# Weight sums of a seven-product scheme: made by DMAs that add to their destination instead of by VectorE

## The chip, the cores and the metric

The kernel runs on one core of one Trainium2 chip. The metric is the device time of one execution in microseconds (us). Of the kernel before, three runs took 2652.19, 2656.02 and 2655.14 us, so the median is 2655.14 us.

## The reference, cut to what matters

The reference is a trunk of two layers on a residual stream of 512 tokens by 1024 features, all in fp32. Each layer runs a gated feed-forward block, a mixer (short convolution beside dilated attention) and a second gated feed-forward block, each on a normed and modulated copy of the stream:

```python
def _swiglu(h, w_gate, w_up, w_down):
    return (jax.nn.silu(h @ w_gate) * (h @ w_up)) @ w_down
```

Here `w_gate` and `w_up` are 1024 x 2816 and `w_down` is 2816 x 1024. There are four such blocks (two layers, two each). Only the products `h @ w_gate` and `h @ w_up` are touched by the change.

## The kernel before, in words

**Split matmuls.** TensorE works on fp32r operands. Every fp32 operand is split into a high part (`hi`, a cast by ScalarE) and a rest (`lo = x - hi`, a subtraction by VectorE), and a product is three matmuls: hi by hi, hi by lo, lo by hi.

**Seven products instead of eight.** For most of the feed-forward's 22 column blocks of 128, two blocks m and m+1 form one group, the class `Seven`. Its weights are two tiles named `raw`, each 128 x 8 x 256, one of `w_gate` and one of `w_up`. Cut into upper and lower 512 rows they give four quarters: a and c (gate), b and d (up). The activations are quartered too. Seven products of sums of quarters replace the eight plain ones. A `Product` casts and subtracts a quarter of 128 x 1024 (lines 539 and 150 of the profile), then runs 24 matmuls of 256 columns (line 550). The sums of activations are made once per block by `Sums.make`; the sums of weights are made for every group by `minus` (line 572), which writes over a quarter in its `raw` tile.

**What sets the order.** In `ffn`, `up` runs over groups and overlaps two of them: while group m runs its products 5, 6, 7, 4 and 3, the next group is loaded and runs its products 1 and 2. A part of two or three groups is followed by `down_part`, which multiplies the finished activations by `w_down`. The framework's scheduler reorders instructions of the several engines by its own estimates, after which every engine works through its list in that order and waits at semaphores. Four `raw` tiles exist (`RAWS = 4`); they hold the two weights of two groups, and `w_down` and the mixer's weights pass through the same four. Loads are issued from the SP queue.

**At the start.** `rows` (line 283) loads small vectors as rows into a tile `rows` of which there are two; TensorE turns them (line 288), VectorE copies them into `vec`. It is called three times: norms and conv weights, the bias `ada_b` of layer 0, that of layer 1.

**POOL** before the change does a few adds of squares for the norms (line 399), a power (354), some modulations (376) and copies in the attention. It issues no DMA.

Of the kernel before, what the change touches and what calls it, by code (L numbers as in the profile page):

```python
# [21 lines left out]
F32 = mybir.dt.float32  # L25
# [5 lines left out]
P = 128  # L31
D = 1024
S = 512
# [87 lines left out]
def trunk(ctx: ExitStack, tc: tile.TileContext, x, c, ada_t, ada_b, norm_g, ffn_w_gate, ffn_w_up, ffn_w_down,  # L121
# [155 lines left out]

    def rows(srcs, col):
        n = sum(s.shape[0] for s in srcs)
        st = sp.tile([P, P], F32, tag="rows", bufs=2, name="rows")  # L280
        at = 0
        for s in srcs:
            nc.scalar.dma_start(st[at:at + s.shape[0]], s)
            at += s.shape[0]

        def end():
            pt = bank("at")
            T.transpose(pt[:, :n], st[:n], ident[:n, :n])
            V.tensor_copy(vec[:, col:col + n], pt[:, :n])

        return end
# [204 lines left out]
    class Sums:  # L496
# [8 lines left out]
        def make(self, i, whole):  # L505

            h11, h21 = whole[:, :4, HALF[0]], whole[:, :4, HALF[1]]
            h12, h22 = whole[:, 4:, HALF[0]], whole[:, 4:, HALF[1]]
            dst, a, b, op = ((h22, h21, h22, ALU.add), (h22, h22, h11, ALU.subtract),
                             (h21, h11, h21, ALU.subtract), (h22, h12, h22, ALU.subtract))[i - 1]  # L510
            V.tensor_tensor(dst, a, b, op=op)
            hi, lo = (v[:, i - 1] for v in self.parts)
            A.copy(hi, dst)  # L513
            sub(lo, dst, f(hi))
# [41 lines left out]
    class Seven:  # L556

        def __init__(self, raw1, raw2, sums, tag="mm"):  # L560
            self.a, self.c = raw1[:, :4], raw1[:, 4:]
            self.b, self.d = raw2[:, :4], raw2[:, 4:]
            self.sums = sums
            self.one, self.two, self.three = bank(tag), bank("at"), None

        def kept(self, src):
            s = F.take()
            A.copy(s.ap, src)  # L568
            return s

        def minus(self, dst, x, y):
            V.tensor_tensor(dst, x, y, op=ALU.subtract)  # L572

        def plus(self, s, src):
            V.tensor_tensor(s.ap, s.ap, src, op=ALU.add)

        def split1(self):
            self.p1 = Product(self.a, quarter(0, 0), self.one, True)

        def split2(self):  # L580
            self.p2 = Product(self.c, quarter(1, 0), self.two, True)
# [5 lines left out]
        def run2(self):  # L587
            self.p2.run()
            self.plus(self.c11, self.two)

        def split5(self, room=None):
            self.minus(self.a, self.b, self.a)
            self.three = bank("o")
            self.p5 = Product(self.a, self.sums(1), self.three, True, room)

        def split6(self):
            self.minus(self.a, self.d, self.a)
            self.p6 = Product(self.a, self.sums(2), self.one)

        def run56(self):  # L600
            self.p5.run()
            self.p6.run()
            self.c12 = self.kept(self.one)

        def split7(self):
            self.minus(self.b, self.d, self.b)
            self.p7 = Product(self.b, self.sums(3), self.one)

        def run7(self):
            self.p7.run()  # L610
# [1 line left out]
            self.plus(self.c22, self.three)  # L612

        def split43(self):
            self.minus(self.c, self.c, self.a)
            self.p4 = Product(self.c, quarter(1, 1), self.one)
            self.p3 = Product(self.d, self.sums(4), self.three)

        def run43(self):
# [4 lines left out]
        def out(self):  # L624
            return self.c11, self.c12, self.one, self.c22

    def first_group(raws):

        sums = Sums()
        group = Seven(*raws, sums, "o")  # L630
        group.split1()
        group.split2()
        group.split5(sums.room())
        return group

# [14 lines left out]
    def gate_up(l, i):  # L650

        held = {}

        def raws(m):
            return [load(w[l, i][:, m * P:(m + 2) * P]) for w in (ffn_w_gate, ffn_w_up)]

        def get(m):
            if m not in held:
                g, u = (halves_of(raw, NC) for raw in raws(m))
                held[m], held[m + 1] = (g[0], u[0]), (g[1], u[1])  # L660
            return held.pop(m)

        get.held, get.raws = held, raws
        return get

    def ffn(l, i, get, first, whole):

        acts = {}
        R.top = N_LOW
        group = first_group(get.raws(len(first) + len(first) % 2))  # L670

        def swiglu(m, pg, pu):
            t = F.take()
            A.activation(t.ap, pg, AF.Silu)  # L674
            V.tensor_tensor(t.ap, t.ap, pu, op=ALU.mult)
            hi, lo = R.take(), R.take()
            A.copy(hi.ap, t.ap)
            sub(lo.ap, t.ap, f(hi.ap))
            t.give()
            acts[m] = hi, lo  # L680

        def swiglu_pair(m, g1, u1, g2, u2):

            A.activation(g1.ap, g1.ap, AF.Silu)
            V.tensor_tensor(u1.ap, u1.ap, g1.ap, op=ALU.mult)
            g1.give()
            s = F.take()
            A.activation(s.ap, g2, AF.Silu)
            V.tensor_tensor(u2.ap, u2.ap, s.ap, op=ALU.mult)
            s.give()  # L690
            hi, lo = R.take(2), R.take(2)
            hv, lv = (s.ap.rearrange("p (c n) -> p c n", c=2) for s in (hi, lo))
            for half, t in enumerate((u1, u2)):
                tv = t.ap.rearrange("p (c n) -> p c n", c=2)
                A.copy(hv[:, :, HALF[half]], tv)  # L695
                sub(lv[:, :, HALF[half]], tv, f(hv[:, :, HALF[half]]))
                t.give()
            acts[m], acts[m + 1] = zip(hi.apart(), lo.apart())

        wv = whole.ap.rearrange("p (k n) -> p k n", k=NC)  # L700
        sums = group.sums
        modulating["phase"] = "up"
        if len(first) % 2:
            for n, banks in enumerate(first):
                swiglu(n, *banks)
            banks = [any_bank() for _ in range(2)]
            for pd, u in zip(banks, get(len(first))):
                project([(pd, u)], h, NC)
            swiglu(len(first), *banks)
        group.run1()  # L710
        group.run2()
        groups = {len(first) + len(first) % 2: group}
        begun = [False]

        def make(i):
            if not begun[0]:
                sums.make(i, wv)

        def up(part):
            modulating["phase"] = "up"  # L720
            late = None
            for m in range(*part):
                if m not in groups:
                    continue
                here, after = groups.pop(m), None
                if not begun[0]:
                    make(1)
                    here.split6()
                    make(2)
                    if len(first) % 2 == 0:  # L730
                        for n, banks in enumerate(first):
                            swiglu(n, *banks)
                else:
                    here.split5()
                    here.split6()
                    if late:
                        swiglu_pair(*late)
                if m + 2 < DFF // P:
                    after = groups[m + 2] = Seven(*get.raws(m + 2), sums)
                    after.split1()  # L740
                here.run56()
                make(3)
                here.split7()
                if after:
                    after.run1()
                    after.split2()
                here.run7()
                here.split43()
                make(4)
                if after:  # L750
                    after.run2()
                here.run43()
                if not begun[0]:
                    begun[0] = True
                    whole.give()
                late = m, *here.out()
                if not after:
                    sums.give()
                    R.top = N_R
            if late:  # L760
                swiglu_pair(*late)

        def rhs(lo):
            return lambda k: (acts[lo + k][0].ap, acts[lo + k][1].ap)

        def down_part(part):
            modulating["phase"] = "down"
            lo, hi = part
            down(ffn_w_down[l, i][lo * P:hi * P], rhs(lo), hi - lo, (l, 2 * i, 2))
            for m in range(lo, hi):  # L770
                for s in acts.pop(m):
                    s.give()

        for part in FF_PARTS[:-2]:
            up(part)
            down_part(part)
        up(FF_PARTS[-2])
        up(FF_PARTS[-1])
        down_part(FF_PARTS[-2])
        lo, hi = FF_PARTS[-1]  # L780

        def give():
            for m in range(lo, hi):
                for s in acts.pop(m):
                    s.give()

        return ffn_w_down[l, i][lo * P:hi * P], rhs(lo), mods[l, 2 * i, 2], give
# [665 lines left out]
```

## Time and profile before

| | |
|---|---|
| median of three runs | 2655.14 us |
| profiled execution, whole | 2655.01 us |
| its span | 2653.2 us |
| PE (matmul) busy | 2615.4 us, 99% |
| DVE busy | 1835.8 us, 69% |
| ACT busy | 1174.3 us, 44% |
| POOL busy | 212.0 us, 8% |
| DMA queue q1, share of 16 engines | 37.3% |

Busy times are read against the span; time outside the span is 1.8 us. A matmul's busy time overlaps that of the next, so the time that PE stands still is read from its waits and from the starts of its instructions.

### The profile page before, as it was taken

What the parts mean: (1) busy time and instruction counts of PE and PEld (TensorE: products, weight loads), DVE (VectorE), ACT (ScalarE), POOL (GpSimd) and SP (SyncE); (2) the same over time, 40 slices, a digit from 0 to 9 for tenths busy, and PEclk for the clock granted to TensorE, in tenths of its full rate; (3) what the DMA queues carried; (4) which work ended last, traced back from release to release, by engine and by line L of the source; (5) the groups of instructions that cost most, each with busy time, mean ns of one, the idle gap of its engine ahead of it and who ended that gap; (6) DMA issues with size and microseconds to landing.
All of it is one profiled execution on the core that took longest, in us unless ns stands there. A gap on an engine that the chain in (4) does not pass through costs nothing. (4 is left out here: it accounts for less than half of the span.)

```text
span 2653.2 us, 40548 instructions
## 1 busy us (share of the span) xinstructions
PE 2615.4 (99%) x16265; PEld 2347.4 (88%) x16265; DVE 1835.8 (69%) x2867; ACT 1174.3 (44%) x2200; POOL 212.0 (8%) x545
## 2 busy tenths in 40 slices
PE   8999999999999999999999999999999999999998
PEld 6899989888888889999999999988888888999998
DVE  8987775675672468877888777756756634777675
ACT  5444454353352345444564445443444423545343
POOL 0000022011010020000020000311112000200001
PEclk9999999999999999999999999999999999999999
DMA  9544143352342224353414423443523422233221
GB/s 328 189 160 129 55 145 120 127 160 87 127 136 87 95 88 145 126 190 101 155 65 167 151 96 114 133 123 98 178 90 118 143 83 84 64 112 101 91 92 68
DMA packets 285480, 326.42 MB, mean 123 GB/s; under 512 B 8057, under 2 KB 263404, under 8 KB 285292
## 3 DMA queue, kind: packets, MB, share of 16 engines
q1 hardware_dynamic: 284980, 323.71, 37.3%
q8 instruction: 127, 2.08, 0.3%
q14 instruction: 61, 0.50, 0.1%
q10 hardware_dynamic: 312, 0.13, 0.0%
HBM read 321.67 MB, written 2.13 MB: 122 GB/s over the span
## 5 line engine op out<-in xcount | busy, mean ns | idle before, releaser
L220 DVE TENSOR_TENSOR slots_r<-raw,slots_r 128x512 fp32r<-128x512 f32 (+1 forms) x584 | 364.9, 644 | 322.3 <-PE mm L241 158.1
L219 ACT CAST slots_r<-raw 128x512 fp32r<-128x512 f32 (+2 forms) x584 | 326.6, 582 | 406.1 <-PE mm L242 174.8
L240 PE MATMUL mm<-hh,slots_r 128*128 128x512 f32 (+1 forms) x1320 | 485.9, 370 | 0.0
L241 PE MATMUL mm<-hl,slots_r 128*128 128x512 f32 (+1 forms) x1320 | 483.1, 367 | 0.5 <-DVE hl L150 0.3
L242 PE MATMUL mm<-hh,slots_r 128*128 128x512 f32 (+1 forms) x1320 | 483.4, 367 | 0.0
L150 DVE TENSOR_TENSOR slots_r<-raw,slots_r 128x1024 fp32r<-128x1024 f32 (+3 forms) x401 | 378.1, 970 | 108.4 <-ACT slots_r L539 40.2
L539 ACT CAST slots_r<-raw 128x1024 fp32r<-128x1024 f32 x273 | 282.6, 1048 | 309.5 <-PE o L242 54.0
L242 PEld LDWEIGHTS mm<-hh,slots_r 128*128 128x128 f32 x1320 | 250.0, 189 | 43.3
L241 PEld LDWEIGHTS mm<-hl,slots_r 128*128 128x128 f32 x1320 | 250.2, 190 | 37.4 <-DVE hl L150 1.1
L240 PEld LDWEIGHTS mm<-hh,slots_r 128*128 128x128 f32 x1320 | 249.0, 190 | 36.4 <-ACT slots_f L674 0.2
L550 PE MATMUL o<-slots_r 128*128 128x256 f32 x2064 | 260.6, 283 | 1.4 <-ACT slots_r L513 1.3
L550 PEld LDWEIGHTS o<-slots_r 128*128 128x128 f32 x2064 | 253.4, 191 | 3.7 <-ACT slots_r L513 1.5
L550 PE MATMUL mm<-slots_r 128*128 128x256 f32 x1680 | 214.4, 283 | 1.4 <-DVE slots_r L150 1.4
L240 PE MATMUL mm<-slots_r 128*128 128x512 f32 (+1 forms) x584 | 212.5, 365 | 2.8 <-ACT slots_r L695 2.8
L241 PE MATMUL mm<-slots_r 128*128 128x512 f32 (+1 forms) x584 | 212.8, 364 | 1.0 <-DVE slots_r L150 1.0
L550 PE MATMUL mm<-hh,slots_r 128*128 128x256 f32 x1120 | 210.7, 280 | 2.2 <-ACT slots_f L568 2.2
L242 PE MATMUL mm<-slots_r 128*128 128x512 f32 (+1 forms) x584 | 212.2, 363 | 0.0
L550 PEld LDWEIGHTS mm<-slots_r 128*128 128x128 f32 x1680 | 206.7, 192 | 3.0 <-DVE slots_r L150 1.6
L572 DVE TENSOR_TENSOR raw<-raw 128x1024 f32<-128x1024 f32 x156 | 190.8, 1229 | 9.4 <-DMA raw<-in_ffn_w_up_dram 7.1
L550 PEld LDWEIGHTS mm<-hh,slots_r 128*128 128x128 f32 x1120 | 176.2, 188 | 4.3 <-ACT slots_f L568 4.2
L550 PE MATMUL mm<-hl,slots_r 128*128 128x256 f32 x560 | 156.3, 279 | 0.0
L399 POOL TENSOR_TENSOR slots_f<-slots_f 128x256 f32<-128x256 f32 x60 | 50.0, 834 | 1115.0 <-ACT slots_f L396 897.2
(197 smaller groups left out, 4540.2 us busy)
## 6 DMA issues: line engine op xcount, KB each, us to landing
slots_f<-in_ada_t_dram SPq DMA_DIRECT2D x144, 512.0 KB, 4.1
raw<-in_w_in_dram SPq DMA_DIRECT2D x52, 1024.0 KB, 6.2
raw<-in_ffn_w_gate_dram SPq DMA_DIRECT2D x42, 1024.0 KB, 5.3
raw<-in_ffn_w_up_dram SPq DMA_DIRECT2D x42, 1024.0 KB, 5.7
raw<-in_ffn_w_down_dram SPq DMA_DIRECT2D x32, 768.0 KB, 4.7
raw<-in_w_in_dram SPq DMA_DIRECT2D x48, 512.0 KB, 5.2
raw<-in_ffn_w_down_dram SPq DMA_DIRECT2D x20, 512.0 KB, 3.5
raw<-in_w_conv_out_dram SPq DMA_DIRECT2D x8, 1024.0 KB, 4.9
```

The costliest lines, as they stand in the source:

```text
L150: V.tensor_tensor(out_, a, b, op=ALU.subtract)
L219: A.copy(hv, src)
L220: (eng or V).tensor_tensor(lv, src, f(hv), op=ALU.subtract)
L240: T.matmul(dst, hi, xh[:, cols], start=first, stop=False)
L241: T.matmul(dst, hi, xl[:, cols], start=False, stop=False)
L242: T.matmul(dst, lo, xh[:, cols], start=False, stop=last)
L399: G.tensor_tensor(acc, acc, sq, op=ALU.add)
L539: A.copy(hv, src)
L550: T.matmul(dst, a, b, start=self.first and k == i == n == 0, stop=True, skip_group_check=True)
L572: V.tensor_tensor(dst, x, y, op=ALU.subtract)
```

## The change

The sums of weights are turned so that each of them is a plain sum that grows in place: b becomes b + w22, then w12 + w22 + w11, then that + w21; a becomes w11 + w12. (The activations' sums and the gated product turn their signs to match.) Each step is one DMA from DRAM with `accum_op=ALU.add`, issued by POOL. `minus` and its four VectorE subtractions per group go: 39 groups, 156 DMAs of 512 KB each. Product 7 is now split first of the products on b, then 6, then 4; c is no longer changed. Further, the space for DMA descriptors grows from 1024 to 4096, and `rows` gets one buffer instead of two.

```diff
-        st = sp.tile([P, P], F32, tag="rows", bufs=2, name="rows")
+        st = sp.tile([P, P], F32, tag="rows", bufs=1, name="rows")
...
-            V.tensor_tensor(dst, a, b, op=op)
+            if i % 2:
+                sub(dst, a, b)
+            else:
+                V.scalar_tensor_tensor(dst, a, -1.0, b, op0=ALU.mult, op1=ALU.subtract)
...
+            self.w11, self.w21, self.w12, self.w22 = get.blocks(m)
+            self.gather(self.b, self.w22)
...
+        def gather(self, dst, src):
+            G.dma_start(dst, src, accum_op=ALU.add)
...
-        def minus(self, dst, x, y):
-            V.tensor_tensor(dst, x, y, op=ALU.subtract)
...
             self.p1 = Product(self.a, quarter(0, 0), self.one, True)
+            self.gather(self.a, self.w12)
...
+        def split7(self):
+            self.p7 = Product(self.b, self.sums(3), self.one)
+            self.gather(self.b, self.w11)
...
         def split5(self, room=None):
-            self.minus(self.a, self.b, self.a)
...
         def split6(self):
-            self.minus(self.a, self.d, self.a)
-            self.p6 = Product(self.a, self.sums(2), self.one)
+            self.p6 = Product(self.b, self.sums(2), self.one)
+            self.gather(self.b, self.w21)
...
-            self.minus(self.c, self.c, self.a)
-            self.p4 = Product(self.c, quarter(1, 1), self.one)
+            self.p4 = Product(self.b, quarter(1, 1), self.one)
...
-            V.tensor_tensor(u1.ap, u1.ap, g1.ap, op=ALU.mult)
+            V.scalar_tensor_tensor(u1.ap, u1.ap, -1.0, g1.ap, op0=ALU.mult, op1=ALU.mult)
...
-                here.split7()
                 if after:
+                    after.split7()
...
-    nc = bacc.Bacc("TRN2", target_bir_lowering=False, num_devices=1, dynamic_dma_scratch_size=1024)
+    nc = bacc.Bacc("TRN2", target_bir_lowering=False, num_devices=1, dynamic_dma_scratch_size=4096)
```

How this moves instructions is shown at three places. Line numbers behind the first edits are higher by 2 to 12 in the changed kernel.

ScalarE's list at the start of the program, before (the three loads of `rows` stand ahead of everything that needs them):

```order
L283 DMA rows<-in_final_g_dram 8x128
L283 DMA rows<-in_ada_b_dram 72x128
L1279 ACTIVATE hl,ssq<-slots_f 128x1024 x4
L1295 ACTIVATE slots_f<-slots_f 128x1024
L283 DMA rows<-in_ada_b_dram 72x128
L1288 COPY xT<-mm 128x4x128 x4
L1300 COPY slots_f<-at 128x512
```

The same piece now:

```order
L285 DMA rows<-in_final_g_dram 8x128
L1291 ACTIVATE hl,ssq<-slots_f 128x1024 x4
L1307 ACTIVATE slots_f<-slots_f 128x1024
L285 DMA rows<-in_ada_b_dram 72x128
L1300 COPY xT<-mm 128x4x128 x4
L285 DMA rows<-in_ada_b_dram 72x128
L1312 COPY slots_f<-at 128x512
```

The first `ada_b` load has moved to where the second stood, and the second behind four more copies; it cannot be issued before TensorE has turned the first.

VectorE's list at the end of a down part in the first layer's second feed-forward, before (`raw_10107` and `raw_10109` are the gate and up weights of the group that comes next):

```order
L150 TENSOR_TENSOR slots_r_69<-raw_9682,slots_r_69 128x1024
L150 TENSOR_TENSOR slots_r_69<-raw_10107,slots_r_69 128x1024
L150 TENSOR_TENSOR slots_r_69<-raw_9680,slots_r_69 128x1024
L150 TENSOR_TENSOR slots_r_69<-raw_9682,slots_r_69 128x1024
L150 TENSOR_TENSOR slots_r_69<-raw_10107,slots_r_69 128x1024
L572 TENSOR_TENSOR raw_10107<-raw_10109,raw_10107 128x1024
L572 TENSOR_TENSOR raw_10107<-raw_10107 128x1024
L150 TENSOR_TENSOR slots_r_69<-raw_10314,slots_r_69 128x1024
L575 TENSOR_TENSOR slots_f_70<-slots_f_70,o_10101 128x512
```

The same place now (`raw_10111` and `raw_10113` are that group's weights):

```order
L152 TENSOR_TENSOR slots_r_69<-raw_10113,slots_r_69 128x1024
L152 TENSOR_TENSOR slots_r_69<-raw_10111,slots_r_69 128x1024
L152 TENSOR_TENSOR slots_r_69<-raw_9686,slots_r_69 128x1024
L152 TENSOR_TENSOR slots_r_69<-raw_10111,slots_r_69 128x1024
L152 TENSOR_TENSOR slots_r_69<-raw_10113,slots_r_69 128x1024
L152 TENSOR_TENSOR slots_r_69<-raw_10318,slots_r_69 128x1024
L583 TENSOR_TENSOR slots_f_70<-slots_f_70,o_10105 128x512
```

The subtractions of line 572 are gone, and the splits stand closer: the two rows that read `raw_10113` are products 7 and 6, between which the DMA that adds w11 has to be issued and land.

POOL's list at the end of the first mixer, before (line 399 sums squares for the norm of the next block, line 354 is the power behind it):

```order
L804 COPY mx0x<-mx_6169 32x2 x16
L804 COPY ng_6496<-top 32x2 x16
L804 COPY sm0x<-sm_6529 32x2 x16
L399 TENSOR_TENSOR slots_f<-slots_f 128x256 x5
L354 TENSOR_TENSOR rs<-rs,minus_half 128x2
L399 TENSOR_TENSOR slots_f<-slots_f 128x256 x5
```

The same place now:

```order
L816 COPY sm0x<-sm_6529 32x2 x16
L575 DMA raw<-in_ffn_w_up_dram 128x4x256 x2
L401 TENSOR_TENSOR slots_f<-slots_f 128x256 x3
L575 DMA raw<-in_ffn_w_up_dram 128x4x256
L401 TENSOR_TENSOR slots_f<-slots_f 128x256 x2
L356 TENSOR_TENSOR rs<-rs,minus_half 128x2
```

Three of the new DMAs stand among the norm's adds, ahead of the power.

## Rows read from the trace of the kernel before

**Rows 1.** Page, part 1: busy time, share of span, instructions, each engine.

```profile
PE 2615.4 (99%) x16265; PEld 2347.4 (88%) x16265; DVE 1835.8 (69%) x2867; ACT 1174.3 (44%) x2200; POOL 212.0 (8%) x545
```

**Rows 2.** Waits of PE: line, waited for, us in total, times, longest.

```profile
PE at L408 <- POOL slots_f L399: 6.1, 4, 2.5
...
PE mm L240 <- ACT slots_r L695: 2.8, 2, 2.3
PE mm L550 <- ACT slots_f L568: 2.2, 3, 1.1
...
PE mm L550 <- DVE slots_r L150: 1.4, 1, 1.4
PE o L550 <- ACT slots_r L513: 1.3, 1, 1.3
PE mm L241 <- DVE slots_r L150: 1.0, 2, 0.8
PE at L550 <- DVE slots_r L150: 0.9, 1, 0.9
```

**Rows 3.** Groups by form: xcount | busy us, mean ns | idle before, releasers.

```profile
L150 DVE TENSOR_TENSOR slots_r<-raw,slots_r 128x1024 fp32r<-128x1024 f32 x273 | 327.5, 1219 | 77.3 <-ACT slots_r L539 40.2 <-PE mm L550 11.9 <-PE o L241 11.1
...
L539 ACT CAST slots_r<-raw 128x1024 fp32r<-128x1024 f32 x273 | 282.6, 1048 | 309.5 <-PE o L242 54.0 <-DVE raw L572 53.4 <-PE o L550 30.0
...
L572 DVE TENSOR_TENSOR raw<-raw 128x1024 f32<-128x1024 f32 x156 | 190.8, 1229 | 9.4 <-DMA raw<-in_ffn_w_up_dram 7.1
...
L385 DVE SCALAR_TENSOR_TENSOR xT<-mm,mod,xT 128x512 f32<-128x512 f32 x72 | 52.3, 746 | 22.1 <-PE mm L242 22.1
L399 POOL TENSOR_TENSOR slots_f<-slots_f 128x256 f32<-128x256 f32 x60 | 50.0, 834 | 1115.0 <-ACT slots_f L396 897.2 <-issue 215.5
...
L685 DVE TENSOR_TENSOR slots_f<-slots_f 128x512 f32<-128x512 f32 x39 | 26.7, 685 | 0.3
```

**Rows 4.** Timeline of PE, 1026 to 1060 us: start, us, what.

```profile
1031.16 5.92 PE L550 MATMUL o<-slots_r 128*128 128x256 f32 x48
1036.93 3.04 PE L550 MATMUL mm<-slots_r 128*128 128x256 f32 x24
```

**Rows 5.** Stretches: length, busy us of PE, PEld, DVE, ACT, POOL, clock, DMA, GB/s.

```profile
80.00:92.00 12.00, 9.14 (x70) 8.33 (x69) 12.00 (x13) 5.55 (x7) 0.00 (x0) 1.00 0.53 183
92.00:96.00 4.00, 4.00 (x22) 4.00 (x22) 4.00 (x7) 2.29 (x5) 0.00 (x0) 0.57 0.86 276
...
300.00:320.00 20.00, 20.00 (x167) 19.75 (x166) 17.55 (x19) 10.26 (x15) 0.00 (x0) 1.00 0.42 138
```

**Rows 6.** DMAs: queue q1's packets, MB, share; issues, KB, us to landing.

```profile
q1 hardware_dynamic: 284980, 323.71, 37.3%
...
slots_f<-in_ada_t_dram SPq DMA_DIRECT2D x144, 512.0 KB, 4.1
...
raw<-in_ffn_w_down_dram SPq DMA_DIRECT2D x20, 512.0 KB, 3.5
```

**Rows 7.** Tile raw: time to landing of all loads into it.

```profile
DMA to landing us min/median/max: 3.0/5.2/11.0
```

**Rows 8.** Timeline of the first 18 us: start, us, what, wait before.

```profile
10.98 0.32 ACTq L283 DMA_DIRECT2D rows<-in_ada_b_dram  x1
...
14.30 1.06 PE L1298 MATMUL at<-ident,rs 128*128 128x128 f32 x4
...
15.40 0.59 ACT L1300 COPY slots_f<-at 128x512 f32<-128x512 f32 x1 [0.27 <-PE at L1298]
...
16.89 0.38 PE L288 MATMUL at<-ident,rows 72*128 72x72 f32 x1 [1.52 <-DMA rows<-in_ada_b_dram]
...
17.96 2.43 PE L1341 MATMUL mm<-hh,slots_r 128*128 128x512 f32 x4 [0.69 <-ACT hh L1313]
```

More of the change, by code (lines that the diff above doesn't have):

```diff
@@ L508, in make @@
             h12, h22 = whole[:, 4:, HALF[0]], whole[:, 4:, HALF[1]]
-            dst, a, b, op = ((h22, h21, h22, ALU.add), (h22, h22, h11, ALU.subtract),
-                             (h21, h11, h21, ALU.subtract), (h22, h12, h22, ALU.subtract))[i - 1]
-            V.tensor_tensor(dst, a, b, op=op)
+            dst, a, b = ((h22, h22, h21), (h22, h22, h11), (h21, h11, h21), (h22, h22, h12))[i - 1]
+            if i % 2:
+                sub(dst, a, b)
+            else:
+                V.scalar_tensor_tensor(dst, a, -1.0, b, op0=ALU.mult, op1=ALU.subtract)
             hi, lo = (v[:, i - 1] for v in self.parts)
@@ L556, in trunk, with __init__ @@
     class Seven:
-        def __init__(self, raw1, raw2, sums, tag="mm"):
+        def __init__(self, get, m, sums, tag="mm"):
+            raw1, raw2 = get.raws(m)
             self.a, self.c = raw1[:, :4], raw1[:, 4:]
             self.b, self.d = raw2[:, :4], raw2[:, 4:]
+            self.w11, self.w21, self.w12, self.w22 = get.blocks(m)
+            self.gather(self.b, self.w22)
             self.sums = sums
             self.one, self.two, self.three = bank(tag), bank("at"), None
+        def gather(self, dst, src):
+            G.dma_start(dst, src, accum_op=ALU.add)
         def kept(self, src):
@@ L603, in run56 @@
             self.c12 = self.kept(self.one)
-        def split7(self):
-            self.minus(self.b, self.d, self.b)
-            self.p7 = Product(self.b, self.sums(3), self.one)
         def run7(self):
@@ L625, in out, with first_group @@
             return self.c11, self.c12, self.one, self.c22
-    def first_group(raws):
+    def first_group(get, m):
         sums = Sums()
-        group = Seven(*raws, sums, "o")
+        group = Seven(get, m, sums, "o")
         group.split1()
         group.split2()
+        group.split7()
         group.split5(sums.room())
@@ L661, in get, with blocks @@
             return held.pop(m)
-        get.held, get.raws = held, raws
+        def blocks(m):
+            return [w[l, i][r * S:(r + 1) * S, m * P:(m + 2) * P].rearrange("(k p) m -> p k m", p=P)
+                    for w in (ffn_w_gate, ffn_w_up) for r in range(2)]
+        get.held, get.raws, get.blocks = held, raws, blocks
         return get
@@ L669, in ffn @@
         R.top = N_LOW
-        group = first_group(get.raws(len(first) + len(first) % 2))
+        group = first_group(get, len(first) + len(first) % 2)
         def swiglu(m, pg, pu):
@@ L688, in swiglu_pair @@
             A.activation(s.ap, g2, AF.Silu)
-            V.tensor_tensor(u2.ap, u2.ap, s.ap, op=ALU.mult)
+            V.scalar_tensor_tensor(u2.ap, u2.ap, -1.0, s.ap, op0=ALU.mult, op1=ALU.mult)
             s.give()
@@ L738, in up @@
                 if m + 2 < DFF // P:
-                    after = groups[m + 2] = Seven(*get.raws(m + 2), sums)
+                    after = groups[m + 2] = Seven(get, m + 2, sums)
                     after.split1()
```

## The prediction

> **What bounds the kernel now.** I read the page's busy times first. PE is busy for 2615.4 us of a span of 2653.2 us, so at most 37.8 us of the span can be won by anything that doesn't shorten matmuls; DVE at 69% is no bound on average [rows 1]. PE's own timeline shows that it isn't only busy but packed: 48 matmuls of 256 columns start in 1036.93 - 1031.16 = 5.77 us, 0.120 us each, and the next product follows without a hole [rows 4]. A product of 24 is then 2.9 us and a group of seven 20.2 us. Next the waits of PE: those that ScalarE and VectorE end with splits, copies and casts come to 9.6 us in the rows shown, the largest 2.8 us in total, against 6.1 us that POOL's adds for the norms cost [rows 2]. So VectorE hardly ever holds PE up. There are two exceptions of degree. Between products VectorE is 17.55 of 20 us busy, and at 80 to 92 us, in the first group of the first feed-forward, it is busy throughout while PE works 9.14 of 12 us; the granted clock then falls to 0.57 in the four us that follow [rows 5]. These are the places where less VectorE work could show.
>
> **The change part by part.** The profiled execution took 2655.01 us, 1.8 us more than its span, and lies 0.1 us under the median, so the sum is made against 2655.0.
>
> *The subtractions that go.* 156 of 1.229 us, 190.8 us of VectorE [rows 3]. PE doesn't wait for most of it. What it can give back is bounded by the 9.6 us of waits on ScalarE and VectorE [rows 2], or, where the clock fell, by that fall as well: 0.43 of 4 us, 1.7 us [rows 5], 11.3 us in all. Below, nothing. Half of this is in the first 100 us or at ends of parts, where gated products and casts follow one another and a lighter VectorE helps only partly; I take 6 us gained, the middle.
>
> *Form of the remaining sums.* 78 gated products and 8 activation sums become scalar-tensor-tensor: 0.746 us against 0.685 us for 512 columns [rows 3], so some 86 x 0.06 = 5 us on VectorE. It is hidden behind the 190.8 us that went; without that cover it would have cost less than 5 us. I count nothing.
>
> *The DMAs that add.* No row of before shows one, nor any DMA of POOL. From below: the same transfer without adding, 512 KB of `w_down` in the same shape, lands 3.5 us after its issue on SP [rows 6]. From above: the slowest load of a `raw` tile, 11.0 us [rows 7]. A value between them: 3.5 us; plus a second passage of the bytes, since the destination must be read too, which is 32 packets for each of 16 engines at 0.373 x 16 x 2653.2 / 284980 = 0.056 us, 1.8 us [rows 6]; plus one short operation's time on POOL for writing out the list of transfers, 0.8 us by its adds [rows 3]. That makes 6.1 us from issue to landing, and it lies nearer to the 3.5 us row, which has the same bytes and shape, than to the 11.0 us one.
>
> What it costs PE is a matter of distance. I counted, in the changed program's common sequence, how many matmuls stand between each of the 156 DMAs and the first matmul that reads the split of the same quarter (512 columns as two), at 0.120 us each. Between them lie the cast, 1.05 us, and the subtraction, 1.22 us [rows 3], so a DMA that takes G hurts PE where the distance is under G + 2.27 us. The median distance is 16.9 us, but the short ones are as short as 4.7 us. The group whose VectorE rows are shown with the change has one of the short ones: from the DMA that adds w11, behind the split of product 7, to product 6's first matmul stand 56 matmuls, 6.7 us. The order supposes a landing within about 3.5 us. At G = 3.5 five DMAs are late, by 3 us together. At 6.1 it is 22, by 40 us together, or 24 us if only the latest of each up part counts (a PE that has once waited gives the others time). At 11.0 it is 51, by 217 or 94 us. I take the middle at 6.1, 32 us.
>
> Queued behind a late one: the cast waits at the head of ScalarE's list, with the copies out of PSUM and the next casts behind it, and its subtraction at the head of VectorE's. 61 of the 156 splits stand closer behind their DMA than 6.1 us. I let the lighter VectorE pay for this and count nothing more. On POOL, three of the new DMAs now stand among the adds of squares before the second feed-forward; the power and with it PE's row sums wait behind them. POOL is 8% busy [rows 1], so its time is not short, but its list is in order: a load that lands late holds the norm. I leave that in the range too.
>
> *The traffic.* 156 x 0.52 = 82 MB on top of 323.7 MB [rows 6]; the DMA share between products is 0.42 [rows 5], and doubling the passage of the new bytes leaves it under 1. Nothing on PE.
>
> *One buffer for `rows`.* Before, the load of layer 1's bias is issued at 10.98 us and PE turns it at 16.89 us, after waiting 1.52 us for it; the first matmul of the feed-forward starts at 17.96 us [rows 8]. Now that place in ScalarE's list belongs to layer 0's bias, and its turning stands on PE ahead of the four transposes that took 14.30 to 15.36 us. These move to about 17.3 us, and only then can layer 1's load be issued, which PE again has to turn before the first matmul. With the same 5.9 us from issue to use it is there at 23.2 us, 5.2 us late. From below, 0: PE's pauses up to 92 us, 2.9 us in one of the stretches alone [rows 5], can swallow part of it and VectorE works on meanwhile. I take 3 us lost.
>
> Sum: 2655.0 - 6 + 32 + 3 = 2684 us.
>
> **A rule weighed against it.** For a DMA issued from POOL the trace of before has no row; for the same bytes from SP it has 3.5 us and 4.1 us [rows 6]. The Trainium skill (DMA: Bandwidth & Descriptors, Anatomy of one DMA) states a fit for POOL's DMAs, 2.0 us plus the bytes over 436 GB/s; an estimate by that page is 3.2 us here, and by it the DMAs would cost PE 3 us or less instead of 32, a sum of about 2655 us. The same page (Rules for kernel authors) says that an accumulating DMA reads its destination and writes it later, which speaks for the second passage and against a plain transfer's time; no run here shows either.
>
> **The rivals.**
>
> *The adding is as cheap as a plain load, and VectorE's relief is felt.* G = 3.5 us, 3 us lost; the start is swallowed by the pauses that follow; the full 11.3 us come back: 2655.0 + 3 - 11 = 2647 us, faster. For it speaks that VectorE is full in the first group and 17.55 of 20 us between products [rows 5]; against it, that PE waits so little for it elsewhere [rows 2].
>
> *Hidden, and nothing gained.* G about 4 us: 8 DMAs late by 7 us together, 3 us at the start, 6 to 8 us back: 2657 us, within 0.2%. For it speaks the median distance of 16.9 us.
>
> *The adding is dear.* Each DMA moves 512 pieces of 1 KB, and POOL may need several us to write the list, with the destination's reading on top. At G = 9 us 38 DMAs are late, by 127 us, or 62 us if one per part counts; at 11.0 us 217 or 94 us. The middle of the four is about 100 us: 2755 us. It decides from the point where three landings and three splits of a group no longer fit between loads: 2 x 5.2 us of loads [rows 7], 3 G and 3 x 2.27 us within the 40.4 us for which four tiles let a pair live, G = 7.7 us. Against it speaks that POOL is otherwise idle in the feed-forward.
>
> **How the numbers follow.** Forecast, G between 5 and 7.5 us: 0.47; its own range is 2665 to 2728 us (by the same count 14 to 19 us lost at 5 us, 41 to 76 us at 7.5 us, each with the 6 us won and the 3 us lost). Cheap and faster: 0.17. Hidden: 0.13. Dear: 0.23. What can be told from no change is about 0.2%, 5.3 us. So faster 0.17, within 0.13, slower 0.70. Downward the range reaches just past the faster rival's 2647 us; of the dear rival it takes in what G of about 9 us costs, and leaves out the rest. The range is 2646 to 2765 us.
>
> **What would show it.** In the profile after: line 572 gone from VectorE and its busy time down by some 185 us; 156 issues on POOL, with a time to landing near 6 us; ScalarE's casts of line 543 waiting for a DMA into `raw`, in total some 100 us; PE waiting for these splits in up parts, 1 to 3 us at a time, about 30 us together, some of them followed by a lower granted clock; the first feed-forward matmul at 21 to 24 us. The forecast is wrong if the landing is under 4 us, or if POOL shows several us for each issue; and wrong in its ground if PE's waits grow at places with no new DMA near.

## The result, and the profile after

The changed kernel is slower: 2791.1 us (2784.8 to 2794.5) against 2653.7 us in the same comparison, a ratio of 1.0515 [1.0493, 1.0537]. The forecast was 2684 us with a range of 2646 to 2765 us: the direction was right, the size was not, and the time lies above the range. The profiled execution has a span of 2788.7 us.

First the page of the changed kernel, as [rows 1, 3 and 6] are of the kernel before: busy times; packets, MB and share of the 16 DMA engines' time; the new issues on POOL; and KB and median us to landing of some DMAs.

```profile
PE 2654.1 (95%) x16265; PEld 2379.5 (85%) x16265; DVE 1658.2 (59%) x2711; ACT 1164.0 (42%) x2200; POOL 407.4 (15%) x701
...
q1 hardware_dynamic: 284980, 323.71, 35.4%
q0 software_dynamic: 82368, 81.80, 19.3%
...
L575 POOL DMA_DIRECT2D raw<-in_ffn_w_up_dram x78 | 103.7, 1376 | 1119.3 <-DVE slots_r L152 578.2
...
raw<-in_ffn_w_gate_dram SPq DMA_DIRECT2D x42, 1024.0 KB, 5.6
raw<-in_ffn_w_up_dram SPq DMA_DIRECT2D x42, 1024.0 KB, 7.0
raw<-in_ffn_w_up_dram POOLq DMA_DIRECT2D x78, 512.0 KB, 6.5
raw<-in_ffn_w_gate_dram POOLq DMA_DIRECT2D x78, 512.0 KB, 6.0
```

VectorE is relieved as meant (1835.8 to 1658.2 us). The adding DMAs land after 6.0 to 6.5 us. PE, though, is idle for 2788.7 - 2654.1 = 134.6 us instead of 37.8, and its same 16265 matmuls take 38.7 us more. Most of that is the clock (mean granted 0.995 before, 0.978 now): PE was busy for 90.8 us at the lower of its two levels, 1.2 GHz, against 21.7 us before, and a matmul takes about twice as long there (shown below), so that half of the difference, 34.6 us, is lost.

What PE waited for (line, releaser, us in total, times, longest), to be held against [rows 2]:

```profile
PE mm L554 <- ACT slots_f L579: 63.7, 26, 7.6
PE at L410 <- POOL slots_f L401: 11.4, 5, 6.8
PE at L290 <- DMA rows<-in_ada_b_dram: 6.9, 2, 5.1
PE o L554 <- ACT slots_r L543: 5.6, 2, 4.7
...
PE mm L554 <- ACT slots_r L543: 5.0, 1, 5.0
...
PE o L554 <- DVE slots_r L152: 4.0, 4, 1.7
...
PE o L554 <- ACT slots_f L579: 3.6, 3, 2.2
```

Line 543 and line 152 are the splits' cast and subtraction. In these rows they hold PE directly for 14.6 us only. Line 579 is `kept`, the copy of a finished product out of PSUM, which needs no DMA at all and frees the bank of the next product: 2.2 us before, 67.3 us now. ScalarE's own waits say what stood ahead of it:

```profile
ACT slots_r L543 <- DMA raw<-in_ffn_w_gate_dram: 131.0, 34, 10.4
ACT slots_r L543 <- DMA raw<-in_ffn_w_up_dram: 103.4, 23, 12.0
```

All 57 of these waits are for adding DMAs. One place where it can be read in full, ScalarE's list (start, us, instruction, idle before and its releaser):

```profile
1156.06 0.60 ACT L700 ACTIVATE slots_f<-mm 128x512 f32<-128x512 f32 x1 [0.31 <-PE mm L554]
1166.64 1.05 ACT L543 CAST slots_r<-raw 128x1024 fp32r<-128x1024 f32 x1 [9.98 <-DMA raw<-in_ffn_w_up_dram]
1167.60 0.61 ACT L707 CAST slots_r<-slots_f 128x512 fp32r<-128x512 f32 x1
1168.12 1.04 ACT L543 CAST slots_r<-raw 128x1024 fp32r<-128x1024 f32 x1
1171.30 0.62 ACT L707 CAST slots_r<-slots_f 128x512 fp32r<-128x512 f32 x1 [2.14 <-DVE slots_f L697]
1171.83 1.99 ACT L543 CAST slots_r<-raw 128x1024 fp32r<-128x1024 f32 x2
1173.72 0.58 ACT L579 COPY slots_f<-mm 128x512 f32<-128x512 f32 x1
```

and PE's at the same time:

```profile
1167.22 0.28 PE L554 MATMUL mm<-hh,slots_r 128*128 128x256 f32 x1
1174.35 4.00 PE L554 MATMUL mm<-slots_r 128*128 128x256 f32 x17 [6.85 <-ACT slots_f L579]
```

The cast stands idle for 9.98 us for a DMA issued at 1157.99 and usable at 1166.64. Behind it stand three more casts, two pieces of the gated product and the copy; the second piece waits another 2.14 us for VectorE, which had itself stood idle for 9.49 us until the first piece came. PE finishes its product at 1167.5 and gets the next bank 6.85 us later; then 17 matmuls take 4.00 us instead of 17 x 0.12 = 2.04. The stretches of this place show why (us, busy of PE, PEld, DVE, ACT, POOL, granted clock, DMA share, GB/s):

```profile
1160.00:1166.00 6.00, 6.00 (x52) 6.00 (x52) 0.00 (x0) 0.00 (x0) 0.00 (x0) 1.00 0.95 221
1166.00:1174.00 8.00, 1.50 (x13) 1.29 (x11) 5.76 (x7) 5.21 (x7) 1.28 (x1) 0.91 0.09 8
1174.00:1178.00 4.00, 3.65 (x17) 3.65 (x18) 1.27 (x2) 0.94 (x2) 0.00 (x0) 0.50 1.12 269
```

The DMA engines are full for six us while ScalarE and VectorE do nothing, then empty while those catch up and PE stands, and after the stand the clock is at its lower level (0.50, 1.2 GHz). I followed all 29 waits of PE for line 579 back along ScalarE's list in this way: for 17 of them, 46.5 of 67.3 us, the last stop at its head was a cast waiting for an adding DMA. For 7 (8.6 us) it was a cast waiting for a plain load, and for 3 (9.7 us), the place shown among them, the gated product waiting for VectorE.

The start went as predicted, for [rows 8] (PE's list):

```profile
23.05 0.35 PE L290 MATMUL at<-ident,rows 72*128 72x72 f32 x1 [5.14 <-DMA rows<-in_ada_b_dram]
23.15 2.91 PE L1353 MATMUL mm<-hh,slots_r 128*128 128x512 f32 x6
```

Where the time is lost is seen best by the start of the n-th matmul (n counted from 0), us later than in the kernel before (worked out from the traces of all kernels here; the columns are the experiments below):

```
  n   before    after    e1     e2     e3     e6     e9     e8
  400   89.6     13.4    9.5    8.2    2.5   11.9    9.5    3.8
 1200  215.3     34.1   17.3   17.4   -0.7   18.2    9.8    6.4
 2000  328.2     42.9   19.1   18.5   -1.2   19.1   10.1    5.9
 5600  990.9     43.3   19.3   19.0   -0.6   22.8   11.1    5.1
 9200 1491.2    106.2   39.4   43.7   -4.8   31.7   11.8    6.8
10800 1727.2    113.7   40.7   43.6   -8.0   31.8   13.0    4.1
13600 2275.6    113.9   41.2   43.9   -7.7   32.9   12.4    4.6
16000 2607.0    135.3   52.1   45.6   -9.0   48.3   19.8    5.0
```

Nearly everything is lost in the feed-forwards, whose groups run in the kernel before from 68 to 347 us, from 985 to 1655 us and from 2293 to 2607 us. Across the mixers between them (rows 2000 to 5600 and 10800 to 13600) the changed kernel loses 0.4 and 0.2 us.

### The profile page after: what moved, and what is told of

Same layout as the page of the kernel before. It is cut to its first block, busy times and chain, and to the rows that moved or that the text cites. A ratio compares the mean times of both kernels' runs of the same rounds, so it can differ in the third digit from the quotient of the medians.

```text
span 2788.7 us, 40980 instructions
## 1 busy us (share of the span) xinstructions
PE 2654.1 (95%) x16265; PEld 2379.5 (85%) x16265; DVE 1658.2 (59%) x2711; ACT 1164.0 (42%) x2200; POOL 407.4 (15%) x701
## 3 DMA queue, kind: packets, MB, share of 16 engines
q1 hardware_dynamic: 284980, 323.71, 35.4%
## 5 line engine op out<-in xcount | busy, mean ns | idle before, releaser
L554 PE MATMUL o<-slots_r 128*128 128x256 f32 x2064 | 267.0, 288 | 15.6 <-ACT slots_r L543 5.6
L554 PE MATMUL mm<-slots_r 128*128 128x256 f32 x1680 | 229.1, 295 | 49.9 <-ACT slots_f L579 49.8
L554 PEld LDWEIGHTS o<-slots_r 128*128 128x128 f32 x2064 | 259.7, 196 | 18.8 <-ACT slots_r L543 6.4
L575 POOL DMA_DIRECT2D raw<-in_ffn_w_up_dram x78 | 103.7, 1376 | 1119.3 <-DVE slots_r L152 578.2
L554 PEld LDWEIGHTS mm<-slots_r 128*128 128x128 f32 x1680 | 219.8, 203 | 54.8 <-ACT slots_f L579 54.8
L575 POOL DMA_DIRECT2D raw<-in_ffn_w_gate_dram x78 | 102.3, 1315 | 447.8 <-DVE slots_r L152 370.9
```

Source lines behind the costliest of these rows:

```text
L554: T.matmul(dst, a, b, start=self.first and k == i == n == 0, stop=True, skip_group_check=True)
L575: G.dma_start(dst, src, accum_op=ALU.add)
```

## The experiments

Two theories stood against each other (the expectations name theories by letters; each says what its letters mean). *Queue*: late DMAs cost little at their own matmuls; they stop ScalarE's and VectorE's lists, and PE waits for work behind them. *Load*: the DMA engines themselves are the trouble, by traffic or by raw tiles that are held longer. They turned out to be two layers of the same loss.

**Another order (e1).** The scheduler is told a landing of about 7 us for POOL's DMAs, where its own price put it near 3.4; every instruction stays.

```
+    hw_specs.TRN2Spec.DMA_START_POOL_CYCLES_SWDGE = 5000.0   (was 700)
```

> The changed kernel with the same instructions, but the scheduler that orders them is told a landing of about 7 us for a DMA issued by POOL instead of about 3.4 us. Theory A (the loss comes from lists ordered for a landing that is too short: ScalarE stands at a cast that waits for a DMA, with the copies out of PSUM behind it): most of the 136 us go, 2655 to 2700 us. Theory B (the DMAs' traffic slows loads, whoever waits): 2770 us or more. Theory C (the landing itself is too long for the chain of three sums of a group, in any order): 2750 us or more.

Measured: 2702.8 us, ratio 1.0178 [1.0159, 1.0196]. That is 3 us above theory A's range and far under those of B and C. By ratios 3.4%, 89 of the 137 us, came from the order alone. PE's waits:

```profile
PE mm L554 <- ACT slots_f L579: 15.2, 12, 3.8
PE at L410 <- POOL slots_f L401: 8.2, 6, 2.5
PE mm L242 <- ACT slots_r L707: 7.7, 5, 3.0
```

The copy's wait fell from 63.7 to 15.2 us with landings as long as before (6.3 and 6.8 us).

**No adding (e2).** The changed kernel's order, DMAs that overwrite; the sums of weight blocks are left out by it.

```
-            G.dma_start(dst, src, accum_op=ALU.add)
+            G.dma_start(dst, src)
```

> The changed kernel with the same order on every engine, but the 156 DMAs of POOL overwrite their destination instead of adding to it (the sums are left out). If reading the destination makes up the landing, as the prediction's 1.8 us had it, the landing falls from 6.0 to 6.5 us to some 4.5 us and the time to 2690 to 2740 us. If the writing of the list on POOL (1.29 us each) and the path make it up, the landing stays over 5.5 us and the time over 2760 us.

Measured: 2695.2 us, ratio 1.0151 [1.0133, 1.0169]. From its page, for q0 and POOL's issues:

```profile
q0 software_dynamic: 22464, 81.80, 9.3%
...
L575 POOL DMA_DIRECT2D raw<-in_ffn_w_up_dram x78 | 59.1, 758 | 1136.5 <-DVE slots_r L152 575.9
...
raw<-in_ffn_w_up_dram POOLq DMA_DIRECT2D x78, 512.0 KB, 4.6
raw<-in_ffn_w_gate_dram POOLq DMA_DIRECT2D x78, 512.0 KB, 4.1
```

The same bytes land after 4.1 to 4.6 us, so adding costs 1.9 us a landing; it makes 528 packets of a DMA instead of 144, 1.29 us of issue on POOL (the median in the changed kernel) instead of 0.76, and 0.193 x 2788.7 / 156 = 3.45 us of all 16 engines instead of 0.093 x 2699.0 / 156 = 1.61. In an order that supposes 3.4 us, some two us less of landing and 1.84 us less of all engines for each DMA give back 3.6%, 97 us, and PE's wait for the copies falls to 14.5 us. This run does not separate the landing from the traffic.

**No DMAs (e3).** The sums are left out altogether; one buffer for `rows` stays.

```
-            G.dma_start(dst, src, accum_op=ALU.add)
+            return
```

> The changed kernel without the 156 DMAs (the sums of weights are left out; products take the quarters as loaded). It shows what VectorE's relief is worth with nothing in its place, the start with one buffer for rows included. Theory A and B alike: 2645 to 2655 us, that is 3 to 5 us lost at the start and 3 to 11 us won. If more than 2665 us, the loss is at the start or in the turned order of the products.

Measured: 2645.4 us, ratio 0.9958 [0.9943, 0.9973]. So VectorE's relief is real: some 11 us (7 to 15 by the interval), with the late start already paid from it. That is what taking all sums off VectorE can win here, before the DMAs that replace them cost anything.

**DMAs that nobody waits for (e4).** The 156 adding DMAs go into quarters that no split reads any more; the sums are left out.

```
+            for w in (self.w22, self.w12):            (behind split2; w11, w21 into a behind split5)
+                G.dma_start(self.c, w, accum_op=ALU.add)
```

> The changed kernel with all 156 adding DMAs, but into quarters that no later instruction reads (c after product 2's split, a after product 5's): the traffic and POOL's work are there, nobody waits for them (the sums are left out). Theory A: within 10 us of the kernel without these DMAs. Theory B: 2740 us or more.

Measured: 2841.2 us, ratio 1.07 [1.0681, 1.072]. By its number this is theory B, but the kernel is not the clean test of traffic that it was meant to be. SyncE's waits and PE's show why:

```profile
SPq L201 <- DMA raw<-in_ffn_w_gate_dram: 519.1, 33, 24.6
```

```profile
PE mm L554 <- ACT slots_f L579: 108.3, 23, 11.0
```

The dead DMAs kept the raw tiles from the next loads (208.9 us of such waits in the changed kernel), the loads came late, and ScalarE's casts for those stopped the same copies: no cast of line 543 waits for an adding DMA here, but 27 wait for plain loads, 141.1 us in all. Followed back as above, 18 of PE's 24 waits for line 579, 82.2 of 113.2 us, have a cast waiting for a plain load as the last stop. It does not separate traffic from tiles held, but it shows that a late load does what a late sum does.

**One buffer for `rows` (e5)**, alone, in the kernel before.

```
-        st = sp.tile([P, P], F32, tag="rows", bufs=2, name="rows")
+        st = sp.tile([P, P], F32, tag="rows", bufs=1, name="rows")
```

> The kernel before with one buffer for rows instead of two, nothing else. Theory A (the start costs what the prediction said, 5.2 us at the first feed-forward matmul, of which pauses later swallow part): 2656 to 2659 us, the first feed-forward matmul near 23.1 us instead of 17.96. Rival B (the later pauses of the first group swallow all of it): 2653 to 2655 us with the same late first matmul. Rival C (the late start shifts the first loads and casts too and the clock falls): 2662 us or more.

Measured: ratio 1.0009 [0.9998, 1.0019], 2.4 us, with the first feed-forward matmul at 23.57 us. Theory A as far as it can be told: the interval just holds no change.

**An order with still more room (e6).** As e1, with 9000 instead of 5000.

> The changed kernel, its scheduler told a landing of some 10 us (9000 cycles) for POOL's DMAs; the same instructions in another order. By the count of distances no DMA is late at a landing of 6.1 us and two at 7 us (at 5000 cycles: 4 and 15; in the changed kernel: 22 and 27). Theory A (what is left of the loss is lists of ScalarE and VectorE held by DMAs that have not landed): some 2660 us, with the waits of ScalarE's casts for these DMAs well under the 98.6 us of e1 and PE's waits for PSUM copies near those of before. Rival B (what is left is buffers: raw tiles are held longer, loads are issued later and land later): no gain over e1, 2695 to 2715 us, SyncE's waits for raw tiles above e1's 276 us. Rival C (traffic of the adding DMAs slows loads): no gain over e1, with up loads still at 7 us or more but SyncE's waits unchanged.

Measured: 2702.2 us, ratio 1.0161 [1.0141, 1.0181], an interval that overlaps e1's. The queue theory alone (A) fails here. Rivals B and C have the time, but neither has its sign: SyncE's waits for DMAs into raw tiles are 269.7 us, not above e1's 276, and `up` loads land after 5.6 us, not 7. PE's wait for the copies is gone, as it said, and others stand in its place:

```profile
PE at L410 <- POOL slots_f L401: 12.0, 5, 5.0
PE mm L242 <- ACT slots_r L707: 11.6, 6, 3.8
...
PE o L554 <- DVE slots_f L583: 4.6, 3, 2.8
...
PE mm L554 <- ACT slots_f L579: 2.3, 2, 2.0
```

The largest wait of the second kind, on ScalarE:

```profile
2570.13 1.14 ACT L221 CAST slots_r<-raw 128x512 fp32r<-128x512 f32 x2 [3.46 <-DMA raw<-in_ffn_w_down_dram]
2571.18 0.59 ACT L700 ACTIVATE slots_f<-mm 128x512 f32<-128x512 f32 x1
2573.01 1.14 ACT L221 CAST slots_r<-raw 128x512 fp32r<-128x512 f32 x2 [1.24 <-DMA raw<-in_ffn_w_down_dram]
2574.05 0.61 ACT L707 CAST slots_r<-slots_f 128x512 fp32r<-128x512 f32 x1
2576.91 0.62 ACT L707 CAST slots_r<-slots_f 128x512 fp32r<-128x512 f32 x1 [2.24 <-DVE slots_f L697]
```

Now plain loads of `w_down` are late, and the gated product that PE needs, cut into pieces by the last two rows, stands behind their casts. In the 42 us up to there four such loads are issued; the trace tells the landing of one, 6.6 us, against a median of 3.5 us in [rows 6]. The five adding DMAs of that stretch land after 6.1 to 9.5 us. The stretch from 1130 to 1230 us, in the kernel before, in the changed one and in e6 (columns as above, the last but one is the DMA share; the changed kernel is some 50 to 60 us behind there, e6 some 26 us, so the work is not quite the same):

```profile
1130.00:1230.00 100.00, 97.73 (x663) 90.45 (x663) 79.27 (x114) 41.85 (x63) 0.00 (x0) 1.00 0.53 175
```

```profile
1130.00:1230.00 100.00, 91.68 (x633) 86.09 (x632) 61.68 (x85) 38.54 (x58) 14.26 (x12) 0.97 0.82 201
```

```profile
1130.00:1230.00 100.00, 100.00 (x711) 94.36 (x710) 69.76 (x94) 45.58 (x67) 17.41 (x14) 1.00 0.96 234
```

PE works on without a pause in e6's stretch, and the DMA engines are nearly full. By an estimate from these traces, a group needs 4 x 3.45 = 13.8 us of all engines for its sums and, at 0.354 x 2788.7 / 323.71 = 3.05 us per MB of q1, 6.4 us for its loads of 2.1 MB: 20.2 us. That is what its seven products take on PE, with `w_down` still to come.

**Splits on POOL (e7).** Cast and subtraction of the quarters that a DMA has added to, on POOL, so that nobody else's list waits for such a DMA.

```
+            if pool:
+                G.tensor_copy(hv, src)
+                G.tensor_tensor(lv, src, f(hv), op=ALU.subtract)
```

> The changed kernel with cast and subtraction of the four split quarters that a DMA has added to on POOL instead of ScalarE and VectorE (312 instructions moved), so that no list of ScalarE or VectorE waits for such a DMA. The count of distances is about that of the changed kernel: at 6.1 us 20 DMAs late, by 34 us together, 26 us one per part. Theory A (the loss comes from copies out of PSUM and casts queued behind a late split): PE's wait for the copies out of PSUM (63.7 us in the changed kernel) falls to some 5 us, PE waits directly for splits of POOL by 25 to 50 us, time 2690 to 2730 us. Rival B (the late splits themselves hold PE, whichever engine makes them): 2780 us or more, since POOL's splits are slower.

Measured: 2946.7 us, ratio 1.1084 [1.1064, 1.1105]. From POOL's rows by line:

```profile
L545 POOL TENSOR_TENSOR slots_r<-raw,slots_r 128x1024 fp32r<-128x1024 f32 x156 | 413.7, 2660 | 31.6 <-DMA raw<-in_ffn_w_up_dram 8.0 <-PE o L558 6.3 <-PE mm L243 4.0
L544 POOL CAST slots_r<-raw 128x1024 fp32r<-128x1024 f32 x156 | 202.2, 1301 | 544.0 <-PE o L243 240.8 <-DMA raw<-in_ffn_w_gate_dram 86.8 <-DMA raw<-in_ffn_w_up_dram 81.6
```

A split there takes 2.66 + 1.30 = 3.96 us instead of 2.27, on the list that also issues the DMAs. PE's wait for the copies fell to 30.1 us, but it waited some 150 us for POOL's splits. The time is in rival B's range, but POOL's list had to hold 616 us of splits that were not there before. It puts another late thing in the place of the first, and decides nothing.

**One of four sums (e8).** Only w12 into `a` by DMA, the other three by VectorE; two buffers for `rows` (the DMA scratch is 2048 bytes for it), the price of e1.

```
+            V.tensor_tensor(self.b, self.b, self.d, op=ALU.add)    (for product 7)
+            V.tensor_tensor(self.b, self.a, self.d, op=ALU.add)    (for product 6)
+            V.tensor_tensor(self.b, self.b, self.c, op=ALU.add)    (for product 4)
```

> Only one of the four sums of a group by an adding DMA (w12 into a; 39 DMAs instead of 156), the other three by VectorE (117 additions of 1.23 us), rows in two buffers, the scheduler told some 7 us. By the count of distances one DMA is late at 6.1 us, by 0.8 us. Theory A (an adding DMA costs only where it is late): 2647 to 2655 us, the same as before or a little faster, since VectorE loses 39 subtractions (48 us). Rival B (each adding DMA costs by its traffic and its place on POOL, whether late or not): a quarter of the 51 us that e1 lost, some 2665 us.

Measured: ratio 1.0015 [1.0005, 1.0025], 4 us. A quarter of e1's loss would have been 12 us, so adding DMAs don't cost in proportion to their number; here the DMA share from 1130 to 1230 us is 0.59. It isn't a gain either; in the table above its trace is 6.4 us late by row 1200 and no later at the end.

**e6 without the adding (e9).** Every list in the order of e6; the DMAs overwrite, so the sums are left out.

> e6 with DMAs that overwrite instead of adding (the sums are left out by it); every engine's order is the same as in e6, no DMA is late by the count of distances in either, and the raw tiles are held by the same instructions. It takes away the adding alone: some 3.4 us of all 16 DMA engines for each of 156 DMAs become about 1.6 us. Theory A (what e6 still loses is traffic: DMA share 0.84 to 0.96 in the feed-forwards, so loads of w_down and gate land late): 2650 to 2668 us, DMA share at 1130 to 1230 us down from 0.96 to about 0.7. Theory B (what e6 still loses is its order: raw tiles held longer and loads issued late): 2690 us or more.

Measured: 2674.3 us, ratio 1.0074 [1.0061, 1.0088].

```profile
1130.00:1230.00 100.00, 100.00 (x712) 94.37 (x711) 67.46 (x94) 44.14 (x66) 9.00 (x12) 1.00 0.68 227
```

The adding alone is 0.87%, 23 of e6's 43 us, in an order in which by the count of distances no sum stands too close: traffic, or landings of loads and sums together, was about half of what was left. (By the trace some sums are late in e6 all the same: line 543's casts wait 27.9 us there for DMAs into raw tiles, 8.4 us in e9.) The other 20 us are neither theory's number. The start explains 2 to 3. By the table e9 is 9.5 us late by row 400 and loses 7.4 us more behind row 13600. SyncE still waits 190.7 us for DMAs into raw tiles before it may load, against 269.7 us in e6, so tiles held longer are the likely rest, but I didn't separate that.

**e8 without the first feed-forward (e10).** There all four sums stay on VectorE. In every feed-forward the first sum of b also moves, from the set-up of the group to the split of product 7.

```
+        get.by_dma = (l, i) != (0, 0)
```

> e8 (one of the four sums by an adding DMA, rows in two buffers), but in the first feed-forward of layer 0 all four sums by VectorE, since e8 lost 4 to 6 us there and nothing after it. Theory A (the loss of e8 is that stretch alone, where the loads already keep the DMA engines busy 0.73 of the time): 5 us under e8, the ratio to before 0.998 to 1.001. Theory B (e8's loss has other grounds, the order that the scheduler makes): the ratio stays at 1.0015.

Measured: ratio 1.0001 [0.9991, 1.001], no difference from the kernel before. The intervals of e8 and e10 overlap, and e10's trace is 3.2 us late at matmul 400 and 4.1 us at 1200 without any adding DMA before there (e8: 3.8 and 6.4 us). So the place of e8's loss is not shown. No version here beats the kernel before; only e3 is below it, and it leaves the sums out.

## Why the prediction was wrong

*The landing.* Right. 6.1 us was built from 3.5 us for a plain transfer, 1.8 us for a second passage and 0.8 us on POOL; measured 6.0 and 6.5 us. The parts: a plain DMA from POOL takes 4.1 to 4.6 us (e2), adding 1.9 us more, the second passage 3.45 - 1.61 = 1.84 us of engine time. The Trainium skill (DMA: Bandwidth & Descriptors, Anatomy of one DMA), by whose fit an estimate was 3.2 us, is below the 4.1 to 4.6 us measured here even without adding; its rule that an accumulating DMA also reads its destination (Rules for kernel authors) agrees with the doubled engine time, 3.45 us against 1.61 us.

*The start.* Right: 23.15 us against 23.2; 2.4 us measured alone (e5) against 3.

*VectorE's relief.* Right in sign, too small: 6 us were taken, e3 shows 11 us, the bound of the sum, with the late start still in it.

*From landing to PE's time.* This step failed. Late sums at their own matmuls were counted at 32 us; the rows show 14.6 us of waits for splits. Of what queues behind them the prediction said: "I let the lighter VectorE pay for this and count nothing more." That term was 67.3 us of waits for the copies out of PSUM alone (65.1 of the 96.8 us by which PE stands longer than before), plus 4.7 us for line 700, an activation that reads PSUM. A lighter VectorE did not pay for it: what waited was the head of ScalarE's list, and in the place shown nothing behind the cast started during its 9.98 us. The 61 splits that stand closer behind their DMA than 6.1 us come nearer than the 22 late matmuls: ScalarE's casts waited 57 times, 234.4 us in all (some 100 us were forecast), and where a bank's copy stood behind, PE waited for the rest of the landing or for the work piled up behind the cast, up to 7.6 us where 1 to 3 us were expected. e1 shows that this is the main cause: with the same instructions and landings no shorter, another order took this wait down to 15.2 us and gave back 89 of 137 us.

*The clock.* The sum had no term for what new stops cost by it; its 1.7 us were for a fall that might go away. After PE's stop of 6.85 us it was at its lower level (0.50), and over the whole program matmuls took 38.7 us more. By and large it follows the idle time (idle and busy us of PE): 37.8 and 2615.4 before, 50.9 and 2622.3 in e9, 72.2 and 2629.5 in e6, 68.4 and 2637.1 in e1, 134.6 and 2654.1 after, 241.7 and 2699.3 in e7.

*The traffic.* Counted at nothing, because a share of 0.42 with the new bytes doubled stays under 1. That sum is wrong where the bytes move: by the prediction's own 1.8 us a passage the four sums of a group take 4 x 2 x 1.8 = 14.4 us of the 20.2 us that the group lasts, a share of 0.71 on top of 0.42. Only as a mean over the program is it small (0.193 measured). From 1130 to 1230 us the share was 0.53 before, 0.82 in the changed kernel and 0.96 in e6. Of the time lost in the changed kernel this is a part that I can't give apart from the queue, since late transfers stop lists; with an order made for them the adding, its landing and its traffic together, is 23 us (e6 against e9).

*POOL's list.* Left in the range; measured 11.4 us of waits at line 410 against 6.1.

*The rivals.* "The adding is dear" came near the time (2755 us) by luck: it needed a landing of 9 to 11 us. (The middle of its four losses is 110 us, not 100.) The cheap and the hidden rival both need a landing of 4 us or less; the fastest adding DMA took 5.6 us.

## What to carry to other kernels

Work that is moved from an engine to a DMA turns a duration into a wait at the head of an in-order list. Count how many consumers stand closer behind their DMA than its landing, and price each by what stands behind it on that engine, above all the copies that free PSUM banks, not by the distance to its own matmul; PE's clock can add to each stop (38.7 us here). Then sum the DMA engines' time per stage (packets times the time of one, and about double where the DMA adds: 3.45 against 1.61 us here) against the stage's length on PE: a mean share says little where a stage alone fills them. Tell the scheduler the measured landing before judging such a change: that alone was worth 3.4% here, and still not enough.

## What was not expected of the hardware

- An adding DMA of 512 KB makes 528 packets against 144 for the same DMA without adding, costs POOL 1.29 us against 0.76 us, and all 16 engines 3.45 against 1.61 us.
- POOL's DMA of plain bytes lands in 4.1 to 4.6 us, against 3.5 us (`w_down`) and 4.1 us (`ada_t`) from SyncE for as many bytes in [rows 6].
- POOL's subtraction of 128 x 1024 takes 2.66 us where VectorE's takes 1.22 us; its cast takes 1.30 us where ScalarE's takes 1.05 us.
- A stretch of 6 us in which the DMA engines are full (0.95) while ScalarE, VectorE and POOL do nothing, followed by one of 8 us with a DMA share of 0.09 in which PE mostly stands: in this place late transfers did not only delay, they made the engines take turns.
